# Holding VectorE and ScalarE to program order through the mixer of a hybrid mLSTM and retention block

## The chip, the cores and the metric

The kernel runs on one core of a Trainium2 chip. The time is the device time of one execution in microseconds (us). Of the kernel before there are three runs and one execution taken by the profiler.

The core's engines each work off their own list of instructions, in order: TensorE (PE in the profile; its weight loads are PEld), VectorE (DVE), ScalarE (ACT), GpSimdE (POOL) and SyncE (SP), which here issues the transfers.

## The reference

One layer of a streaming encoder, in fp32, on 1024 tokens of width 1024 with 16 learned meta tokens put in front. Four heads are mLSTM heads (a matrix memory with exponential gates), four are retention heads (rotary q and k, fixed decay). All eight have q and k of 128 columns, v of 256 columns and an output gate of 256 columns.

```
y = rmsnorm(x) @ w_in          # q, k, v, output gates, input and forget gates
mLSTM:     h = (intra-chunk scores * exp gates) @ v + decayed state; then / max(|den|, exp(-m))
retention: h = (q k^T * decay) @ v + q_d @ state; rotary on q and k first
mix = head_norm(h) * sigmoid(gate)   # silu(gate) for retention
x = x + mix @ w_out
out = x + gated MLP(x) with a causal depthwise convolution
```

## The kernel before, in words

Every fp32 product is made of three matmuls on rounded halves: hi times hi, low times hi, hi times low (lines 770 to 772). The halves come from a cast on ScalarE (L363, `hi_..`) and a subtraction on VectorE (L368, `lo_..`). On top of that the big products are done with seven block products in place of eight, so sums of weight blocks are made on VectorE (L441 to L446) and sums of input blocks S1 to S4 are split into halves at L1621 and L1622 (`uS4h`, `uS4l`).

The part between the input norm and the output product is called the mixer here. Head by head, in the order 4, 0, 1, 2, 3, 5, 6, 7, TensorE runs a q/k product (`pq0` and so on), a gate product (`po0`), and for each pair of heads one v product (`pv0`, `pv1`, `pv2`). The first one after the set-up is head 4's gate product `po4`. Each product writes into PSUM banks `x` and `y`, which ScalarE (L838, L840) and VectorE (L842) empty into SBUF several times per product; TensorE's next block needs the bank emptied. Beside the product of one head runs the chunked scan of the head before it: nine chunks of scores `s`, state updates `u`, outputs `n`, then transposes `tr` (L1482) of the normalised outputs, scaled by the gate on VectorE into `mx` (L1490). For the retention heads VectorE and ScalarE also rotate q and k (L1037 to L1042), with tables that are loaded into the buffers A1 and A2 (L964, L965, `A<-rot_d`). Those two buffers held the sum S4's source until the split at L1622 has read it. For the mLSTM heads the gates (L1071 to L1138) are a long chain of small steps on all three engines. In the background, pieces of the output weights are also combined on VectorE (L513 to L517, `raw_w`).

The order of the work is set in two layers. A planner in the Python program (`slot`, `go`, `tick`) emits one piece of TensorE work, then side tasks as long as the estimated load of VectorE and ScalarE is not more than 2.5 us ahead of TensorE's. `watch` (L93) sees each instruction as it is emitted and keeps these estimates in `load`, from a small table of rates. Then a scheduler of the framework reorders each engine's instructions by its own estimate of their timing when the program is built. A manual dependency of the kind NoSync binds two instructions of one engine to the order in which they were emitted, without a semaphore. `watch` makes such a chain where `pinned[0]` is true, and in the kernel before it never is: the lists that the engines get are the scheduler's.

Of the kernel before, what the change touches and what calls it, by code (L numbers as in the profile page):

```python
# [65 lines left out]
def body(ctx, tc, h_in, vecs, cst, mask_in, rot, w_v0, w_vp, w_g, w_out, w_up, w_gate, w_down, out):  # L66
# [18 lines left out]
    G, PE, V, AC = nc.gpsimd, nc.tensor, nc.vector, nc.scalar  # L85
    pinned = [False]
    load = {"PE": 0.0, "DVE": 0.0, "Activation": 0.0, "slot": 0.0}
    RATE = {"PE": (0.004, 0.000445), "DVE": (0.12, 0.00098), "Activation": (0.1, 0.00083)}
    before = {}
# [3 lines left out]
    def watch(ins):  # L93
        nm, kind = ins.engine.name, type(ins).__name__
        if nm not in RATE or not ins.outs or "DMA" in kind or "Tile" in kind:
            return
        if pinned[0] and nm in before:
            tc.add_manual_dep(ins, before[nm], mybir.DependencyInfo(mybir.DependencyClass.NoSync, mybir.DependencyReason.DATA), reason="order")
        before[nm] = ins.name
        b, c = RATE[nm]  # L100
        n = c * math.prod(x[1] for x in ins.outs[0].ap[1:])
        if nm == "Activation":
            f = ins.func.name if hasattr(ins, "func") else "Copy"
            if f in TABLES and f != table[0]:
                table[0] = f
                load[nm] += 1.3
        if nm != "PE":
            load[nm] = max(load[nm], load["slot"]) + b + n
        elif F32 in [x.dtype for x in ins.ins]:
            load[nm] += max(0.11, 2 * n) * (0.5 if ins.outs[0].ap[0][1] == 32 else 2)  # L110
        else:
            load[nm] += max(0.11, b + n)
# [731 lines left out]
    def wino_fm(kind, h, chunks, dst):  # L844
        get = gbanks(f"{kind}{h}")
        steps = []
        for n, (b, xb_) in enumerate(ROWS):
            for ci, (j0, j1) in enumerate(chunks):
                def step(n=n, b=b, xb_=xb_, ci=ci, j0=j0, j1=j1):
                    w = need((kind, h, n))  # L850
                    u = UB[xb_]
                    pt = get(b, ci)[:, :j1 - j0]
                    mm3s(pt, [tuple(x[:, k * P:(k + 1) * P] for x in w) for k in range(4)],
                         [tuple(x[:, k, j0:j1] for x in u) for k in range(4)], n in (0, 1, 3), n in (1, 5, 6))
                    o, d = dst(n, j0, j1)
                    defer(lambda: evac(n, d, pt[:, o:]))
                steps.append(step)
        return steps
# [5 lines left out]
    def fm_dst(tiles, keep=0):  # L864
        def dst(n, j0, j1):
            f, half = QUAD[n]
            o = max(0, 16 - j0) if half else 0
            t0 = half * 512 + j0 + o - keep
            return o, tiles[f][:, t0:half * 512 + j1 - keep]
        return dst  # L870
# [4 lines left out]
    def o_steps(h):  # L875
        return wino_fm("o", h, OC, fm_dst([sigt[:, 0], sigt[:, 1]], KEEP))
# [666 lines left out]
    def slot(m, lim=2.5, most=2, pe=1):  # L1543
        load["slot"] = load["PE"]
        if pend or evacs or front:
            tick()
        m()
        pes = 0
        for _ in range(most):
            if not able() or side[0][1] and pes == pe or max(load["DVE"], load["Activation"]) - load["PE"] > lim:  # L1550
                break
            pes += one()

    def go(steps, pe=1):
        for m in steps:
            slot(m, pe=pe)
# [102 lines left out]
    reset()  # L1659
    load.update({"DVE": 4.0, "Activation": 2.0})  # L1660
    done["tr"] = 0.0
    go(o_steps(4))
    pinned[0] = False
    for p, (a, b) in enumerate(PAIRS):
        side += sig_tasks(prev) if p else sig_tasks(4)
        side += rest[0] + loads_of(a)
# [677 lines left out]
```

## Time and profile before

| | |
|---|---|
| runs | 1553.6, 1558.11, 1556.64 us; median 1556.64 us |
| profiled execution | 1557.89 us, span 1556.1 us |
| TensorE busy | 1503.2 us, 97% of the span |
| VectorE busy | 1076.8 us, 69% |
| ScalarE busy | 772.4 us, 50% |
| mean granted TensorE clock | 0.987 |
| the stretch from the first gate product to the last transposes | about 75 to 746 us from the span's start |

Read it by TensorE's idle time and its clock: an engine at 97% leaves 53 us of idle time in all, and what a change of order can win or lose lies there and in the stretches where the granted clock is below 1.

### The profile page before, as it was taken

Reading aid. Unit: us, or ns where it says so; the run is one execution under the profiler, and the core shown is the slowest. Engines: PE = TensorE matmul, PEld = TensorE weight load, DVE = VectorE, ACT = ScalarE, POOL = GpSimd, SP = SyncE. Lnnn points to the kernel's source line nnn. Section 1 sums busy time; section 2 is a strip of 40 time slices with the busy share of each in tenths; the row PEclk is TensorE's granted clock in tenths of the full one; section 3 lists DMA queues with packets and bytes.
Section 4 is the critical chain, followed back from the end, with each engine's and each line's share of the span. In section 5 each row is a group of like instructions: output and inputs, shape, how many; then the busy total and the mean of one; then the engine's idle time right before and its main releaser. Section 6 shows DMA issues by size and latency. Waiting matters only on the chain.

```text
span 1556.1 us, 25506 instructions
## 1 busy us (share of the span) xinstructions
PE 1503.2 (97%) x9929; PEld 1359.0 (87%) x9929; DVE 1076.8 (69%) x2107; ACT 772.4 (50%) x1467; POOL 73.8 (5%) x133
## 2 busy tenths in 40 slices
PE   7999798999999999999999999999999999999997
PEld 6999698889889999997787988999999999888887
DVE  7785767666677567755767788777666666778657
ACT  5464556664666345635345465444444444444443
POOL 1000000000000000000000001222220000000000
PEclk9999899999999999999999999999999999999999
DMA  6032245323632345489332327888773223933313
GB/s 228 1 109 69 96 114 171 106 86 123 185 115 80 112 154 199 163 304 338 131 109 102 126 71 239 215 204 197 190 190 89 82 82 118 379 119 109 99 43 109
DMA packets 104586, 223.81 MB, mean 144 GB/s; under 512 B 10520, under 2 KB 33760, under 8 KB 104288
## 3 DMA queue, kind: packets, MB, share of 16 engines
q1 hardware_dynamic: 95872, 199.02, 38.7%
q0 software_dynamic: 8448, 23.07, 7.5%
q8 instruction: 78, 1.28, 0.3%
q14 instruction: 44, 0.36, 0.1%
q10 hardware_dynamic: 144, 0.07, 0.0%
HBM read 178.05 MB, written 67.15 MB: 158 GB/s over the span
## 4 chain that ended last, share of the span: by engine, by line
PE 78%; DMA 10%; DVE 8%; ACT 3%; issue 1%; SPq 0%; DVEq 0%; ACTq 0%
PE pdx L772 3%; PE pdx L771 3%; PE pdx L770 3%; PE pup_x L771 2%; PE pup_x L772 2%; PE pup_x L770 2%; PE pga_x L770 2%; PE pga_x L771 2%; PE pga_x L772 2%; DMA raw_w<-w_out_d 2%; PE pdy L772 2%; PE pdy L771 2%; PE pdy L770 2%; PE pwx L772 2%; PE pwx L770 2%; PE pwx L771 2%
## 5 line engine op out<-in xcount | busy, mean ns | idle before, releaser
L654 ACT CAST hi_up<-raw_up 128x512 fp32r<-128x512 f32 (+1 forms) x52 | 36.4, 719 | 107.7 <-PE pga_z L771 61.0
L770 PE MATMUL pup_x<-uh_g,hi_up 128*128 128x256 f32 (+1 forms) x240 | 67.7, 284 | 1.2 <-ACT uh_g L1755 1.2
L771 PE MATMUL pup_x<-ul_g,hi_up 128*128 128x256 f32 (+1 forms) x240 | 67.8, 284 | 0.1
L655 DVE TENSOR_TENSOR lo_up<-raw_up,hi_up 128x512 fp32r<-128x512 f32 (+1 forms) x52 | 41.2, 809 | 37.5 <-ACT hi_up L654 36.8
L655 DVE TENSOR_TENSOR lo_ga<-fraw_ga,hi_ga 128x512 fp32r<-128x512 f32 (+1 forms) x52 | 41.8, 808 | 36.2 <-ACT hi_ga L654 36.1
L772 PE MATMUL pup_x<-uh_g,lo_up 128*128 128x256 f32 (+1 forms) x240 | 66.6, 284 | 0.0
L655 DVE TENSOR_TENSOR lo_d<-rd,hi_d 128x1024 fp32r<-128x1024 f32 (+1 forms) x34 | 37.7, 1112 | 32.8 <-ACT hi_d L654 32.7
L654 ACT CAST hi_ga<-fraw_ga 128x512 fp32r<-128x512 f32 (+1 forms) x52 | 36.5, 719 | 44.1 <-PE pup_z L771 23.1
L772 PE MATMUL pdx<-uh_d,lo_d 128*128 128x512 f32 (+1 forms) x156 | 57.9, 375 | 0.0
L771 PE MATMUL pdx<-ul_d,hi_d 128*128 128x512 f32 (+1 forms) x156 | 57.8, 374 | 0.0
L654 ACT CAST hi_d<-rd 128x1024 fp32r<-128x1024 f32 (+1 forms) x34 | 32.3, 959 | 48.7 <-PE pdy L771 32.5
L772 PE MATMUL pdy<-uh_d,lo_d 128*128 128x512 f32 x132 | 51.9, 393 | 0.0
L771 PE MATMUL pdy<-ul_d,hi_d 128*128 128x512 f32 x132 | 51.8, 392 | 0.0
L770 PE MATMUL pdx<-uh_d,hi_d 128*128 128x512 f32 (+1 forms) x156 | 48.5, 372 | 0.0
L770 PE MATMUL pdy<-uh_d,hi_d 128*128 128x512 f32 x132 | 47.9, 389 | 0.0
L770 PEld LDWEIGHTS pup_x<-uh_g,hi_up 128*128 128x128 f32 x240 | 45.8, 191 | 2.3 <-ACT uh_g L1755 1.4
L770 PE MATMUL pga_x<-uh_g,hi_ga 128*128 128x512 f32 x120 | 47.5, 396 | 0.0
L771 PE MATMUL pga_x<-ul_g,hi_ga 128*128 128x512 f32 x120 | 47.5, 396 | 0.0
L772 PE MATMUL pga_x<-uh_g,lo_ga 128*128 128x512 f32 x120 | 47.2, 393 | 0.0
L771 PEld LDWEIGHTS pup_x<-ul_g,hi_up 128*128 128x128 f32 x240 | 45.8, 191 | 1.0 <-DVE ul_g L1756 0.3
L772 PEld LDWEIGHTS pup_x<-uh_g,lo_up 128*128 128x128 f32 x240 | 45.1, 190 | 0.8
L536 POOL DMA_DIRECT2D wsd<-w_down_d x33 | 18.5, 617 | 483.8 <-DVE s2up L1983 476.9
(1684 smaller groups left out, 5794.2 us busy)
## 6 DMA issues: line engine op xcount, KB each, us to landing
raw_up<-w_up_d SPq DMA_DIRECT2D x22, 512.0 KB, 4.2
fraw_ga<-w_gate_d SPq DMA_DIRECT2D x22, 512.0 KB, 4.1
acts<-cv SPq DMA_DIRECT2D x44, 256.0 KB, 4.3
wsd<-w_down_d POOLq DMA_DIRECT2D x44, 256.0 KB, 6.1
rd<-wsd SPq DMA_DIRECT2D x22, 512.0 KB, 3.5
raw_w<-w_out_d SPq DMA_DIRECT2D x20, 512.0 KB, 4.0
wsw<-raw_w SPq DMA_DIRECT2D x32, 256.0 KB, 2.0
raw_m<-w_out_d SPq DMA_DIRECT2D x14, 512.0 KB, 5.1
```

The source lines that it names most:

```text
L536: dep(G.dma_start(x, y), last["pace"], True)
L654: AC.copy(hi[:, o:o + n], x)
L655: V.tensor_tensor(lo[:, o:o + n], x, hi[:, o:o + n].bitcast(F32), ALU.subtract)
L770: m.append(PE.matmul(pt, ah, xh_, start=first and k == 0, stop=False, skip_group_check=True))
L771: PE.matmul(pt, ah, xl_, start=False, stop=False, skip_group_check=True)
L772: m.append(PE.matmul(pt, al, xh_, start=False, stop=last and k == n - 1, skip_group_check=True))
```

## The change

Three edits in `watch` and around the first gate product. `pinned[0]` becomes true just before head 4's gate product, with the chain started afresh by `before.clear()`, and stays true until the mixer's end, where the line `pinned[0] = dealt[0] = False` stood already. In `watch` the chain leaves TensorE out, so only VectorE and ScalarE (the engines that have a rate there beside PE) are held to the order in which the planner emits; TensorE, and the issue of transfers, stay with the scheduler. And each activation that has more than one input (a bias or scale read from memory) adds 0.15 us to the planner's estimate of ScalarE's load. The instructions are the same but for loads of activation tables, which are placed by the order of ScalarE's functions: 44 in the program before, 31 now. Line numbers of the changed kernel are 2 higher behind `watch`, 3 higher after the call of head 4's gate product.

```diff
--- before.py
+++ after.py
@@ -94,12 +94,14 @@
         nm, kind = ins.engine.name, type(ins).__name__
         if nm not in RATE or not ins.outs or "DMA" in kind or "Tile" in kind:
             return
-        if pinned[0] and nm in before:
+        if pinned[0] and nm in before and nm != "PE":
             tc.add_manual_dep(ins, before[nm], mybir.DependencyInfo(mybir.DependencyClass.NoSync, mybir.DependencyReason.DATA), reason="order")
         before[nm] = ins.name
         b, c = RATE[nm]
         n = c * math.prod(x[1] for x in ins.outs[0].ap[1:])
         if nm == "Activation":
+            if len(ins.ins) > 1:
+                load[nm] += 0.15
             f = ins.func.name if hasattr(ins, "func") else "Copy"
             if f in TABLES and f != table[0]:
                 table[0] = f
@@ -1659,8 +1661,9 @@
     reset()
     load.update({"DVE": 4.0, "Activation": 2.0})
     done["tr"] = 0.0
+    pinned[0] = True
+    before.clear()
     go(o_steps(4))
-    pinned[0] = False
     for p, (a, b) in enumerate(PAIRS):
         side += sig_tasks(prev) if p else sig_tasks(4)
         side += rest[0] + loads_of(a)
```

The first place is VectorE at the start of head 4's gate product. `uS4l` is the low half of S4, whose source lies in the buffers of the rotary tables `A`; `sig<-sig,po4y` empties one of the gate product's banks; `qT`, `kT` and `rawq` with `A` are the rotation of head 4; `pvm` is a small side product. Before:

```order
L1622 TENSOR_TENSOR uS4l<-s_0_849,uS4h 128x1056
L785 TENSOR_TENSOR vz<-pvm_0_1139,vz 16x256
L1075 TENSOR_TENSOR gates<-gates 36x128
L1622 TENSOR_TENSOR uS4l<-s_1_850,uS4h 128x1056
L368 TENSOR_TENSOR lo_o_6_0_977<-raw_o4a,hi_o_6_0_976 128x512
L842 TENSOR_TENSOR sig<-sig,po4y_950 128x256
L785 TENSOR_TENSOR vz<-pvm_0_1139,vz 16x256
L1086 TENSOR_SCALAR gates<-gates 36x128
L368 TENSOR_TENSOR lo_o_6_0_977<-raw_q0a,hi_o_6_0_976 128x512
L1080 TENSOR_SCALAR gates<-gates 36x128
L1040 TENSOR_TENSOR qT_908<-rawq,A_4_877 128x528
L1040 TENSOR_TENSOR qT_908<-rawq,A_4_877 128x512
```

In the changed kernel:

```order
L1624 TENSOR_TENSOR uS4l<-s_0_849,uS4h 128x1056
L1624 TENSOR_TENSOR uS4l<-s_1_850,uS4h 128x1056
L1042 TENSOR_TENSOR qT_908<-rawq,A_4_877 128x528
L1043 TENSOR_TENSOR kT_909<-kT_909,A_4_878 128x528
L1044 TENSOR_TENSOR qT_908<-qT_908,kT_909 128x528
L1073 TENSOR_SCALAR gsm<-vec 36x1
L1075 TENSOR_SCALAR gates<-pg,vec 36x128
L1076 TENSOR_SCALAR gates<-gates 36x128
L1077 TENSOR_TENSOR gates<-gates 36x128
L844 TENSOR_TENSOR sig<-sig,po4y_916 128x258
L1042 TENSOR_TENSOR kT_909<-rawk,A_4_877 128x528
L1043 TENSOR_TENSOR rawq<-rawq,A_4_878 128x528
```

The two splits now stand next to each other with the rotation directly behind them, and the emptying of the bank `po4y_916` stands behind three rows that need the tables and four of the gates. Before, it stood seven rows ahead of the piece shown, and an emptying of the second bank `po4y_950`, weight halves and gate steps stood between the splits and the rotation.

The second place is VectorE in head 1's q/k product. `mx` is the scaled transpose, for which TensorE's next transpose waits; `raw_w` is the combining of output weights. Before:

```order
L842 TENSOR_TENSOR rawq<-rawq,pq1y_2604 128x264
L513 TENSOR_TENSOR raw_w_2676<-raw_w_2676,raw_w_2674 128x512
L1441 BN_STATS bn_8_2551<-v_01_2088 128x6
L514 TENSOR_TENSOR raw_w_2674<-raw_w_2674 128x512
L1456 TENSOR_TENSOR z_2_2571<-den_2006 128x2
L1490 TENSOR_SCALAR mx_0_0_2649<-tr_0_0_2642,vec,sig 128x386
L1442 BN_AGGR mv_2_2509<-bn_8_2551 128x2
L368 TENSOR_TENSOR lo_q_5_0_2602<-raw_q1b,hi_q_5_0_2601 128x512
L368 TENSOR_TENSOR lo_q_5_0_2602<-raw_q1a,hi_q_5_0_2601 128x512
L516 TENSOR_TENSOR raw_w_2674<-raw_w_2674,raw_w_2676 128x512
L1457 TENSOR_TENSOR z_2_2571<-z_2_2571,cols 128x2
```

In the changed kernel:

```order
L370 TENSOR_TENSOR lo_q_5_0_2599<-raw_q1b,hi_q_5_0_2598 128x512
L844 TENSOR_TENSOR rawq<-rawq,pq1y_2621 128x264
L1492 TENSOR_SCALAR mx_0_0_2667<-tr_0_0_2660,vec,sig 128x386
L370 TENSOR_TENSOR lo_q_5_0_2599<-raw_q1a,hi_q_5_0_2598 128x512
L1492 TENSOR_SCALAR mx_0_1_2692<-tr_0_1_2686,vec,sig 128x386
L515 TENSOR_TENSOR raw_w_2646<-raw_w_2646,raw_w_2644 128x512
L516 TENSOR_TENSOR raw_w_2644<-raw_w_2644 128x512
L1492 TENSOR_SCALAR mx_1_0_2717<-tr_1_0_2712,vec,sig 128x384
L518 TENSOR_TENSOR raw_w_2644<-raw_w_2644,raw_w_2646 128x512
L519 TENSOR_TENSOR raw_w_2646<-raw_w_2646,raw_w_2644 128x512
L370 TENSOR_TENSOR lo_o_0_0_2698<-raw_o1a,hi_o_0_0_2697 128x512
```

The first `raw_w` row stood four rows ahead of the first `mx`; now it stands behind the second.

The third place is VectorE at the mixer's end. `wa` and `mm` are the scaled transposes of the last head, `resid` adds output products to the residual. Before:

```order
L1490 TENSOR_SCALAR wa_8267<-tr_1_0_8262,vec,sig 128x258
L1284 TENSOR_TENSOR resid_8121<-resid_8121,pwx_8131 128x512
L1284 TENSOR_TENSOR resid_8121<-resid_8121,pwx_8146 128x512
L1148 TENSOR_TENSOR rr_8351<-wa_8369,rr_8351 128x512
L1284 TENSOR_TENSOR resid_8122<-resid_8122,pwx_8162 128x512
L1284 TENSOR_TENSOR resid_8122<-resid_8122,pwx_8178 128x512
L1490 TENSOR_SCALAR wa_8243<-tr_1_1_8272,vec,sig 128x126
L1490 TENSOR_SCALAR wa_8267<-tr_1_1_8272,vec,sig 128x258
L1247 TENSOR_SCALAR wa_8369<-wa_8369,wa_8389 128x512
L655 TENSOR_TENSOR lo_w_2_8483<-raw_w_2_8280,hi_w_2_8482 128x1024
L1490 TENSOR_SCALAR wa_8267<-tr_2_0_8290,vec,sig 128x254
L1490 TENSOR_SCALAR mm<-tr_2_0_8290,vec,sig 128x2
```

In the changed kernel:

```order
L1492 TENSOR_SCALAR wa_8267<-tr_1_0_8262,vec,sig 128x258
L657 TENSOR_TENSOR lo_w_4_8277<-raw_w_4_8117,hi_w_4_8276 128x1024
L1150 TENSOR_TENSOR rr_8352<-wa_8369,rr_8352 128x512
L1246 TENSOR_SCALAR wa_8369<-wa_8369,wa_8362 128x512
L1492 TENSOR_SCALAR wa_8243<-tr_1_1_8272,vec,sig 128x126
L1492 TENSOR_SCALAR wa_8267<-tr_1_1_8272,vec,sig 128x258
L1150 TENSOR_TENSOR rr_8351<-wa_8369,rr_8351 128x512
L1249 TENSOR_SCALAR wa_8369<-wa_8369,wa_8389 128x512
L1492 TENSOR_SCALAR wa_8267<-tr_2_0_8290,vec,sig 128x254
L1492 TENSOR_SCALAR mm<-tr_2_0_8290,vec,sig 128x2
L1492 TENSOR_SCALAR wa_8267<-tr_2_1_8298,vec,sig 128x254
L1492 TENSOR_SCALAR mm<-tr_2_1_8298,vec,sig 128x2
```

The four `resid` rows between the transposes of the last head are gone from here; they follow behind the last `mm`.

## The prediction

> **What bounds the kernel now.** I read the page first, for the shares of the engines, then the table of TensorE's waits over the stretch that the change touches (75 to 760 us), then the table of stretches for the granted clock, and last the rows in order of time where a wait ends.
>
> ```profile
> span 1556.1 us, 25506 instructions
> PE 1503.2 (97%) x9929; PEld 1359.0 (87%) x9929; DVE 1076.8 (69%) x2107; ACT 772.4 (50%) x1467; POOL 73.8 (5%) x133
> ```
>
> TensorE is the bound: 1556.1 - 1503.2 = 53 us idle in all. VectorE and ScalarE have room on average, so their order matters only where TensorE waits for one of them.
>
> ```profile
> engine line waited for: us in total, times, longest us
> PE tr L1482 <- DVE mx L1490: 8.5, 6, 2.3
> PE tr L1482 <- ACT v4lo L1473: 4.7, 1, 4.7
> PE pq3x L770 <- ACT rawq L838: 2.6, 1, 2.6
> PE pq1x L770 <- ACT rawq L838: 2.2, 1, 2.2
> PE tr L1482 <- DVE mm L1490: 1.8, 1, 1.8
> PE tr L1482 <- DVE wa L1490: 1.8, 1, 1.8
> PE pq2x L770 <- DVE rawk L842: 1.7, 2, 1.3
> PE pq0y L772 <- DVE lo_q L368: 1.6, 1, 1.6
> PE pv0y L770 <- ACT v L840: 0.9, 1, 0.9
> ```
>
> These rows and six smaller ones make 29.6 us of waiting in the mixer: the most that a better order there could win back, apart from the clock.
>
> ```profile
> core 0: us, PE busy (x) PEld busy (x) DVE busy (x) ACT busy (x) POOL busy (x), PEclk, DMA share, GB/s
> 75.00:100.00 25.00, 23.25 (x200) 22.09 (x199) 23.46 (x45) 17.33 (x32) 2.44 (x2) 1.00 0.37 127
> 170.00:180.00 10.00, 3.62 (x12) 2.35 (x13) 9.31 (x21) 7.53 (x12) 0.10 (x1) 0.60 0.13 51
> 180.00:190.00 10.00, 10.00 (x70) 8.94 (x70) 5.50 (x17) 4.21 (x9) 0.32 (x2) 0.89 0.14 47
> 240.00:250.00 10.00, 5.66 (x28) 5.42 (x29) 6.39 (x16) 4.81 (x12) 0.18 (x1) 0.68 0.51 134
> 410.00:420.00 10.00, 6.92 (x47) 6.47 (x46) 5.14 (x16) 6.65 (x19) 0.18 (x1) 0.89 0.64 191
> 420.00:430.00 10.00, 10.00 (x79) 9.86 (x78) 7.31 (x20) 7.14 (x13) 0.00 (x0) 0.94 0.85 286
> 735.00:746.00 11.00, 7.32 (x24) 5.40 (x23) 7.92 (x15) 2.56 (x4) 0.00 (x0) 0.69 0.79 280
> ```
>
> Before PEclk stands the busy time of each engine. The first row matters most: in head 4's gate product VectorE is busy 23.46 of 25 us, so it is nearly the bound there. The others show four places where TensorE's clock falls after a cluster of idle time. With a granted clock of 0.5 in those spells, 0.60 of 10 us means 8 us at half clock, 0.89 means 2.2 us, 0.68 means 6.4, 0.69 of 11 us means 6.8, and 0.89 with 0.94 means 3.4. Half of TensorE's busy time in a spell is lost: by my count of the rows about 2.9 us in head 0's v product, 2.5 in head 1's q/k product (240 to 250), 1.7 in head 3's (410 to 430), 2.8 at the mixer's end.
>
> [...]
>
> **The change part by part.** The instructions stay the same, so each term is a wait that comes or goes. I laid the changed lists of the engines beside each other and put the durations of the rows on them.
>
> *First gate product, a loss.* VectorE now meets the rotation directly behind the split of S4, whose buffers the tables are loaded into.
>
> ```profile
> 81.45 0.41 DVE L842 TENSOR_TENSOR sig<-sig,po4y 128x258 f32<-128x258 f32 x1
> 83.48 1.18 DVE L1622 TENSOR_TENSOR uS4l<-s,uS4h 128x1056 fp32r<-128x1056 f32 x1
> 85.24 1.24 DVE L1622 TENSOR_TENSOR uS4l<-s,uS4h 128x1056 fp32r<-128x1056 f32 x1
> 89.80 1.31 DVE L1040 TENSOR_TENSOR qT<-rawq,A 128x528 f32<-128x528 f32 x2 [0.94 <-DMA A<-rot_d]
> 92.14 0.71 DVE L1041 TENSOR_TENSOR kT<-kT,A 128x528 f32<-128x528 f32 x1 [0.44 <-DMA A<-rot_d]
> 84.74 0.33 SPq L964 DMA_DIRECT2D A<-rot_d  x1
> 86.51 0.33 SPq L965 DMA_DIRECT2D A<-rot_d  x1
> 83.77 0.28 PE L770 MATMUL po4y<-uS1h,hi_o 128*128 128x258 f32 x1
> ```
>
> The tables are issued 0.1 us after each split and land 5.1 and 5.6 us later. Before, VectorE filled that time and waited only 0.94 and 0.44 us; the emptying of `po4y` was done at 81.9, and TensorE used the bank at 83.8. Now nothing stands between: with the splits some 1.7 us earlier (rows moved behind them) the second table lands about 90.4, three steps of 0.7 and four gate steps of about 0.25 follow, and the bank comes free near 92. TensorE has work until about 85.2 (83.8 and one more block of 1.4 us). It waits 6 us. Behind that stand the gate chain between `pe` and `pf` (which has no TensorE work in between now; some ten small steps, which I take as 1.65 us together) and single waits of 1.3, 0.55, 0.45 and 0.7 us: 10.65 us. Then the next weights are late: `raw_q0b` was issued at 87.1 and combined at 95.0, 8 us later with 5.9 us of flight.
>
> ```profile
> 87.11 0.80 SPq L239 DMA_DIRECT2D raw_q0b<-w_g_d  x2
> 95.02 0.68 DVE L441 TENSOR_TENSOR raw_q0b<-raw_q0b 128x512 f32<-128x512 f32 x1
> raw_q0b<-w_g_d SPq DMA_DIRECT2D x2, 256.0 KB, 5.9
> ```
>
> It goes into the slot of `raw_o4a`, and on SyncE it now stands behind the gate tables' transfers as well. By the changed order that slot is read out at about 108, so VectorE waits some 3.7 us for the transfer and TensorE 3 + 1 us. In all 14.65 us idle. For the clock I take 4 us, since a cluster of 8.9 us in head 0's v product cost 2.9. Away go the 1.6 us before `pq0y` and a wait of 0.7. Term: 14.65 + 4.0 - 2.3 = +16.3. Bounds: 0 if the tables land in time, 24 if each wait is half as long again.
>
> *Head 0's v product, a gain.* Before, head 4's scan ends in this product:
>
> ```profile
> 173.15 0.47 PE L1482 MATMUL tr<-cs,v4lo 128*128 128x128 f32 x1 [4.70 <-ACT v4lo L1473]
> 176.90 0.48 PE L1482 MATMUL tr<-cs,v4lo 128*128 128x128 f32 x1 [2.28 <-DVE mx L1490]
> L441 DVE TENSOR_TENSOR raw_vp<-raw_vp,raw_vp 128x1024 f32<-128x1024 f32 x3 | 3.7, 1225 | 6.4 <-DMA raw_vp<-w_vp_d 6.4
> ```
>
> With 1.0 and 0.9 us beside these that is 8.9 us, with the clock 11.8. In the changed order the scan runs beside the q/k product before it, and its transposes are done early in the v product. There the pair L441 and L442 (1.2 us each) stands between two `mx` and ahead of a weight half, which I count as 4.8 us, plus 0.85 for a score that waits for the gate, plus 2.5 of clock: 8.15. Term: -3.7, bounds -11.8 and +4.
>
> *The other two v products, a loss.* Before they idle 3.3 us together with no loss of clock. The same pair of L441 and L442 ahead of an `mx` gives 3.2 us in each now, and 1.7 of clock (one spell of 3.4 us). Term: 9.8 - 3.3 = +6.5, bounds -3.3 and +10.
>
> *Heads 1 and 3, q/k product, a gain.*
>
> ```profile
> L513 DVE TENSOR_TENSOR raw_w<-raw_w,raw_w 128x512 f32<-128x512 f32 x8 | 5.5, 693 | 23.8 <-DMA raw_w<-w_out_d 23.8
> 243.19 0.69 DVE L513 TENSOR_TENSOR raw_w<-raw_w,raw_w 128x512 f32<-128x512 f32 x1 [6.27 <-DMA raw_w<-w_out_d]
> 245.47 0.28 PE L1482 MATMUL tr<-cs,vz 16*128 16x16 f32 x1 [2.25 <-DVE mx L1490]
> ```
>
> VectorE stands 6.27 us before a transfer of output weights with the `mx` of head 1 behind it. The changed order has that `mx` first. ScalarE's `rawq` rows, which TensorE awaited for 2.2 and 2.6 us, now come close together, ahead of the exponentials and their table loads. Before: 2.2 + 2.25 + 2.5 = 7.0 in head 1, and 2.6 + 0.5 + 1.7 = 4.8 in head 3. After, one `mx` row of 0.6 and a little: 0.7 each. Term: -10.4, bounds -11.8 and 0.
>
> *The mixer's end, a gain.* The rows on `wa` and `mm` above, 1.8 us each, are transposes that wait behind residual adds:
>
> ```profile
> 735.46 1.28 DVE L1284 TENSOR_TENSOR resid<-resid,pwx 128x512 f32<-128x512 f32 x2
> ```
>
> With the clock 3.7 + 2.8 = 6.5. The adds now come later, and one wait of about 0.75 stays. Term: -5.7, bounds -6.5 and 0.
>
> *Table loads.* 13 loads of an activation table fall away.
>
> ```profile
> L1461 ACT ACT_TABLE_LOAD x11 | 14.1, 1283 | 0.2
> ```
>
> 13 x 1.283 = 16.7 us of ScalarE, which is idle half of the time: costed at nothing, beyond what the `rawq` rows above hold. The dearer activations only move a few side tasks by one piece of TensorE work: nothing either. TensorE itself is not chained, so its list fits itself to the other two: nothing.
>
> *The other products.* Held to order, VectorE can meet a late transfer with a bank behind it. Bounds: -4 (the small waits of before all go) and +14 (rival two). I take +1, one more wait like the 0.94 us before L1040, which is the same kind of wait.
>
> Sum: 16.3 - 3.7 + 6.5 - 10.4 - 5.7 + 1 = +4.0. The profiled execution took 1557.9 us (span 1556.1 and 1.8 around it), so 1561.9; it stands 1.25 above the median of the three runs, against which the sum gives 1560.6. I forecast 1561. What this kernel's runs can tell from no change is about 0.3%, 4.7 us.
>
> **The rivals.** *One: faster.* The rotary tables land before VectorE needs them, or TensorE gets other work placed there by its free scheduler. The point that decides is whether the second table has landed by about 85, against 92.14 before; for it speaks that 7 us of VectorE's work could still be drawn forward, against it that the split rows themselves set the issue. The gate term then shrinks from 16.3 to about 1, the sum to -11: 1546.
>
> *Two: much slower.* Each of the remaining 11 products gets one in-order wait of about 1.3 us (the banks' emptyings or weight halves behind a transfer; the 23.8 us over eight rows of L513 show how long VectorE can stand there): 14 us in place of 1, so 1574 to 1576. It decides if the planner, which counts the load of engines but sees no transfer's landing, runs ahead of the transfers in the steady heads as well. Against it: `raw_q0b` apart, the weights are issued 8 to 10 us ahead in the changed order, and flights like the 5.9 us above fit in.
>
> *Three: no change.* Terms cancel within 4.7 us, or the scheduler's order was near the planner's anyway: about 1557.
>
> *Four: clock lost only to long gaps.* If idle spells of 1 to 3 us cost no clock, the 2.5, 1.7 and 1.7 us that I count for the changed kernel's three v products fall out of the sum: 1561 - 5.9 = 1555. It decides whether a cluster of short waits is enough; the spell at 240 to 250 us (2.2 and 2.25 us idle, clock 0.68) speaks against it. [...]
>
> **How the numbers follow.** Forecast (1556 to 1567) 0.38, of it 0.24 slower by over 4.7 us and 0.14 within; rival one 0.26, of it 0.25 faster; rival two 0.22, all slower; rivals three and four 0.14, of it 0.09 within and 0.05 faster. Faster 0.30, same 0.24, slower 0.46. The range reaches to both outer rivals, 1546 to 1577; the likeliest case's own range is 1556 to 1567.
>
> **What would show it.** Right: TensorE waits 5 to 7 us on `po4y` near 85 to 92 us with VectorE before it on `A<-rot_d`; a clock below 1 there; `pq0` starting some 10 to 12 us later than the 95.6 us of before's first `pq0y` row; no wait of VectorE on `raw_w` with an `mx` behind it near 240 us; the rows of `tr` on `wa` and `mm` nearly gone. Wrong: no wait on the tables, or waits on `lo_` and bank rows spread through heads 2 to 7.

## The result and the profile after

The changed kernel takes 1625.39 us (median of 4 runs, 1622.98 to 1629.85) against 1556.24 us before (median of 4): a ratio of 1.0449, 95% interval 1.042 to 1.0478. The forecast was 1561, 1546 to 1577. The change is slower by 69 us.

The page of the changed kernel:

```profile
span 1620.8 us, 25436 instructions
PE 1525.0 (94%) x9929; PEld 1373.6 (85%) x9929; DVE 1090.2 (67%) x2107; ACT 751.3 (46%) x1454; POOL 72.0 (4%) x133
```

TensorE's instructions are the same 9929. The span grew by 64.7 us. TensorE's idle time grew from 52.9 to 95.8 us (+42.9), its busy time by 21.8, most of it lost to the clock: the mean granted clock fell from 0.987 to 0.976, about 19 us of work at full clock. ScalarE is 21 us less busy (13 table loads of 1.283 us are 16.7 of it), and the time grew all the same.

TensorE's waits over the mixer (75 to 810 us), the largest:

```profile
engine line waited for: us in total, times, longest us
PE po4y L772 <- DVE sig L844: 10.6, 1, 10.6
PE tr L1484 <- DVE mx L1492: 8.4, 8, 2.3
PE pvm L596 <- DMA raw_vm<-w_vp_d: 8.1, 4, 2.6
PE s L1376 <- DVE pt L1400: 5.5, 4, 4.0
PE pv7y L772 <- ACT v7t L842: 3.6, 1, 3.6
PE pq3y L772 <- ACT rawk L842: 3.1, 1, 3.1
PE pq1y L772 <- ACT rawk L842: 2.9, 1, 2.9
PE pv0x L772 <- ACT hi_vp L365: 2.8, 1, 2.8
PE tr L1484 <- DVE wa L1492: 2.3, 2, 1.5
```

One large wait at the gate product and many small ones spread over all heads. VectorE's three largest waits in the same stretch, and that for `raw_w`:

```profile
engine line waited for: us in total, times, longest us
DVE mx L1492 <- PE tr L1484: 56.1, 27, 3.7
DVE pt L1400 <- ACT kw L1392: 34.1, 22, 4.7
DVE bn L1443 <- ACT v L1439: 33.0, 31, 4.5
DVE raw_w L515 <- DMA raw_w<-w_out_d: 7.9, 4, 3.2
```

The rows on the same things in the kernel before (75 to 800 us):

```profile
DVE raw_w L513 <- DMA raw_w<-w_out_d: 23.8, 8, 6.3
DVE pt L1398 <- ACT kw L1390: 13.6, 14, 2.5
DVE bn L1441 <- ACT v L1437: 8.0, 9, 1.3
DVE wa L1490 <- PE tr L1482: 1.6, 3, 0.8
```

VectorE's row on `tr` before `mx` is new. In the kernel before, VectorE's waits for `tr` come to 1.6 us in all (three rows of `wa` at the end). Now it stands 27 times before an `mx` until TensorE has run the transpose. In these 56.1 us TensorE isn't idle: by the trace it runs matmuls of the products for 47.0 us, and the transposes themselves for most of the rest. The waits for `kw` and `v`, scan results that pass through TensorE and ScalarE, have grown; the wait for the transfers of `raw_w` has shrunk.

By the starts of the products in the two traces, the stages took (us; a stage runs from the first matmul of its product to the first of the next):

| stages | before | after | difference |
|---|---|---|---|
| head 4's gate product, head 0's q/k and v products | 119.3 | 134.4 | +15.1 |
| heads 1 and 3, q/k product | 59.0 | 68.5 | +9.5 |
| the other two v products | 95.9 | 104.5 | +8.6 |
| heads 0 and 2, gate product | 69.8 | 78.5 | +8.7 |
| head 6's and 7's products | 135.2 | 158.8 | +23.6 |
| the others in the mixer | 185.9 | 188.2 | +2.3 |
| all behind the mixer | 816.0 | 813.7 | -2.3 |

How it goes in one place, head 1's q/k product, in order of time on ScalarE, TensorE and VectorE:

```profile
268.67 0.62 ACT L365 CAST hi_o<-raw_o1a 128x512 fp32r<-128x512 f32 x1 [5.03 <-DMA raw_o1a<-w_g_d]
269.20 0.65 ACT L842 ACTIVATE rawk<-pq1y 128x248 f32<-128x248 f32 x2
```

```profile
269.62 0.50 PE L772 MATMUL pq1y<-uS4h,hi_q 128*128 128x264 f32 x1 [2.89 <-ACT rawk L842]
269.92 0.42 PE L773 MATMUL pq1y<-uS4l,hi_q 128*128 128x264 f32 x1
270.14 0.42 PE L774 MATMUL pq1y<-uS4h,lo_q 128*128 128x264 f32 x1
...
273.94 0.28 PE L773 MATMUL pq1y<-uS4l,hi_q 128*128 128x264 f32 x1
274.06 0.28 PE L774 MATMUL pq1y<-uS4h,lo_q 128*128 128x264 f32 x1
274.19 0.49 PE L1484 MATMUL tr<-cs,v 128*128 128x128 f32 x3
```

```profile
274.71 0.62 DVE L1492 SCALAR_TENSOR_TENSOR mx<-tr,vec,sig 128x384 f32<-128x384 f32 x1 [3.71 <-PE tr L1484]
275.25 0.40 DVE L844 TENSOR_TENSOR rawk<-rawk,pq1x 128x248 f32<-128x248 f32 x1
```

ScalarE stands 5.03 us before a cast of weights that are still on their way, with the emptying of `pq1y` behind it. TensorE waits 2.89 us for that bank, then runs the 24 matmuls that its own list has there (the first ones at half clock, 0.22 us from start to start against 0.12 later), and only then the transpose. VectorE, held, waits 3.71 us for this transpose, with the next bank behind it.

Around the single wait of 2.89 us TensorE was busy, and the granted clock was 0.50 from 269.74 to 273.15 us. In the kernel before, with two waits of 2.23 and 2.25 us that ended at 242.09 and 245.47 us, it was 0.50 from 243.62 to 250.45 us.

### The profile page after: what moved, and what is told of

Read it like the earlier page. It is cut to its first block, busy times and chain, and to the rows that moved or that the text cites. A ratio compares the mean times of both kernels' runs of the same rounds, so it can differ in the third digit from the quotient of the medians.

```text
span 1620.8 us, 25436 instructions
## 1 busy us (share of the span) xinstructions
PE 1525.0 (94%) x9929; PEld 1373.6 (85%) x9929; DVE 1090.2 (67%) x2107; ACT 751.3 (46%) x1454; POOL 72.0 (4%) x133
## 4 chain that ended last, share of the span: by engine, by line
PE 82%; DVE 6%; DMA 5%; ACT 4%; issue 1%; SPq 0%; DVEq 0%; ACTq 0%
PE pdx L774 3%; PE pdx L773 3%; PE pdx L772 2%; PE pup_x L773 2%; PE pup_x L774 2%; PE pga_x L772 2%; PE pup_x L772 2%; PE pga_x L773 2%; PE pga_x L774 2%; PE pwx L774 2%; PE pdy L774 2%; PE pdy L773 2%; PE pwx L772 2%; PE pdy L772 2%; PE pwx L773 2%; PE pv L812 2%
## 5 line engine op out<-in xcount | busy, mean ns | idle before, releaser
L1492 DVE SCALAR_TENSOR_TENSOR mx<-tr,vec,sig 128x386 f32<-128x386 f32 (+2 forms) x42 | 24.0, 572 | 60.3 <-PE tr L1484 56.1
```

What stands on the lines that cost most here:

```text
L1492: return V.scalar_tensor_tensor(dst, tr[:, x0 - t0:x1 - t0], vec[:, g:g + 1], sig(b, p)[:, x0 - a0:x1 - a0], ALU.mult, ALU.mult)
```

## The experiments

Theory A: what costs is that the lists of the engines come from two hands, VectorE's and ScalarE's from the planner and TensorE's from the scheduler. Theory B: a held engine stands before whatever lands late, whoever orders TensorE. The diffs are against the changed kernel; where a diff is one line, it stands in place of that line of `watch`. Ratios are to the kernel before, measured beside each, and a loss in us is a median less the median of the kernel before beside it (1553.2 to 1556.2); for the changed kernel it is 69.2 us.

**All three engines held.**

```diff
-        if pinned[0] and nm in before and nm != "PE":
+        if pinned[0] and nm in before:
```

> TensorE is held to the planner's order too, the rest as in the changed kernel (1625.4 us). Theory A, two orders at odds: the changed kernel loses its 69 us mainly because VectorE and ScalarE follow the planner while TensorE follows the scheduler, so VectorE stands before mx for a tr that TensorE runs late (48.4 us of such waits between 200 and 780 us). With one order for all three most of that goes: 1560 to 1585, the 10.6 us wait on po4y at the gate product staying. Theory B, head of line: a held engine stands before whatever lands late, transfers above all, whoever orders TensorE: 1615 to 1640, no better.

Measured 1583.36 us, ratio 1.0195 (1.0173 to 1.0218). The loss is 29.6 us: holding one more engine makes the kernel 40 us faster. VectorE's waits for `tr` (75 to 810 us, as in the view above):

```profile
DVE mx L1492 <- PE tr L1484: 20.8, 17, 2.9
```

56.1 became 20.8. Theory B falls as the main cause; it may stand for part of the 30 us that stay. Against the expectation the wait on `po4y` went too: in its place TensorE waited 14.6 us before `pe`, a step of the gates.

**Only VectorE held.**

```diff
+        if pinned[0] and nm in before and nm == "DVE":
```

> Only VectorE is held, ScalarE and TensorE are free. Theory A: VectorE at tr is the cause, so most of the loss stays: 1600 to 1625. Theory B: the loss splits between the two held engines by their waits on late inputs: about half, 1585 to 1600. Either way the wait on the rotary tables at the gate product stays, about 10 us of TensorE idle near 85 us.

Measured 1613.06 us, ratio 1.0386 (1.0367 to 1.0405): 59 of the 69 us, as theory A said. The wait on `po4y` near 85 us was 5.7 us here and not 10. (In this run the two large weight transfers were issued ahead of both rotary tables; see the last section.)

**Only ScalarE held.**

```diff
+        if pinned[0] and nm in before and nm == "Activation":
```

> Only ScalarE is held. Theory A: little is lost, 1555 to 1570. Theory B: ScalarE stands before casts whose weights land late (5.0 us before hi_o from raw_o1a at 263 us, 5.2 in head 3) with bank rows behind: 1580 to 1600. The two single times of VectorE and ScalarE add up to the 69 us if they act alone, and to much less if they lock each other.

Measured 1554.37 us, ratio 1.0002 (0.9988 to 1.0016): nothing against the kernel before, some 5 us against none held (the next run). The two single losses, 59.3 and 0.6 us, make 60 of the 69. The stages show that this is a sum of a loss and a gain: head 4's gate product and head 0's q/k product 28 us longer, head 0's v product 29 us shorter.

**The dearer activations alone.**

```diff
+        if False:
```

> The dearer activations alone, nothing held to order. Both theories: within 0.3% of the kernel before, 1552 to 1561; the prediction costed this edit at nothing.

Measured 1549.62 us, ratio 0.9977 (0.9966 to 0.9988). The edit by itself is a small gain of about 4 us, and this is the fastest kernel of the study. It leaves 36 table loads of 44, and no single stage gains more than 1.6 us.

**The scaled transposes out of the chain.** Only the rows `mx`, `wa` and `mm` are left to the scheduler.

```diff
-        if pinned[0] and nm in before and nm != "PE":
+        if pinned[0] and nm in before and nm != "PE" and not free[0]:
...
+                free[0] = True
+                r = V.scalar_tensor_tensor(dst, tr[:, x0 - t0:x1 - t0], ...)
+                free[0] = False
```

> As the changed kernel (1625.4 us), but the rows that scale the transposes (mx, wa, mm) are left out of VectorE's chain, so the scheduler places them. Theory A in its narrow form, the mx rows before a late tr are what TensorE pays for: 1580 to 1600. Theory A in its wide form, any row of the held list that reads what TensorE makes late (bank rows, C behind u, pt behind s) does the same: 1605 to 1622, since the other rows stand as before.

Measured 1610.0 us, ratio 1.0361 (1.0326 to 1.0395): a loss of 56.2 us, 13 less. The waits did not go:

```profile
DVE mx L1495 <- PE tr L1486: 51.8, 26, 6.2
```

The narrow form of theory A falls. The place of `mx` in VectorE's list isn't what makes it wait; what makes it wait is how late TensorE runs the transpose: of these 51.8 us TensorE spent 41.9 in matmuls of the products.

**Head 4's rotation held back.**

```diff
         def rotary(i, r):
             a, b = HR[r]
+            while h == 4 and not rush[0] and load["PE"] < 14:
+                yield
```

> As the changed kernel, but the planner holds head 4's rotation back until 14 us of TensorE work of the gate product are planned, so the emptying of the gate product's banks and the next weights stand ahead of the rows that need the tables. The wait of 10.6 us on po4y goes if the tables are its cause. The prediction's gate term says 16 us less: 1606 to 1612. If the gates, which now start as late, only move the wait into head 0's q/k product: 1618 to 1628.

Measured 1617.43 us, ratio 1.0411 (1.0382 to 1.044): a loss of 63.7 us, 5.5 less than the changed kernel (8 by the bare medians): between the two expectations and nearer the second. The wait on `po4y` is gone and head 4's gate product takes 22.4 us in place of 38.8, so the tables were its cause. But head 0's v product then takes 5.9 us more and its gate product 7.4 us more: of the 16.4 us most came back in later stages.

**The chain only into head 0's v product.** The line stands behind the first 13 of that product's 28 steps, so the chain ends in the middle of it, not at its end, where the expectation below puts it.

```diff
         drain(f"V{p}")
+        pinned[0] = False
```

> The chain ends at the end of head 0's v product, the rest of the mixer is left to the scheduler. This measures what the part up to head 0's second gate product costs by itself: by the stages of the two traces 15 us (134.4 against 119.3 us), so 1565 to 1573, and 50 to 55 us of the loss lie in the heads after it. If the late heads only suffer from the late start: 1595 or more.

Measured 1566.29 us, ratio 1.0087 (1.0053 to 1.012): a loss of 12.5 us, in the lower part of what was expected. Some 57 us lie behind.

**The chain only from behind head 4's gate product.**

```diff
-    pinned[0] = True
-    before.clear()
     go(o_steps(4))
+    pinned[0] = True
+    before.clear()
```

> The chain starts only after head 4's gate product. With 12.5 us measured for the chain up to head 0's v product alone, the rest of the 69 us stays if the parts add: 1605 to 1615, a little less if head 0's gains in the v product were part of the 12.5. If the start sets the heads off their pace for good: under 1590.

Measured 1611.68 us, ratio 1.0375 (1.0338 to 1.0413): the loss stays without the start, 58.5 us. With the 12.5 of the run above that is 71, against 69: the two parts add. Both hold head 0's q/k product and the first part of its v product, so this is a rough sum.

**TensorE and VectorE held, ScalarE free.**

```diff
+        if pinned[0] and nm in before and nm != "Activation":
```

> TensorE and VectorE are held, ScalarE is free. Theory A, the pair of TensorE and VectorE must have one order and ScalarE's matters little: 1575 to 1592, as with all three held (1583.4 us). If the three orders must all be one, so that a free ScalarE does to the pair what a free TensorE did: 1600 or more.

Measured 1587.1 us, ratio 1.022 (1.0188 to 1.0252): as with all three. ScalarE's order matters little.

**Only TensorE held.**

```diff
+        if pinned[0] and nm in before and nm == "PE":
```

> Only TensorE is held to the planner's order, VectorE and ScalarE are free. If any two orders at odds cost as much as the changed kernel's: 1590 or more. If it is a held VectorE that costs, since TensorE is the bound and the scheduler can fit the others to it: 1545 to 1565, near the kernel with the dearer activations alone (1549.6).

Measured 1585.42 us, ratio 1.0206 (1.0175 to 1.0237). Neither expectation holds. The planner's order of TensorE alone costs 32 us, and holding the other two as well adds nothing (29.6). Its waits are of another kind: TensorE waits for `mx`, hardly VectorE for `tr` (75 to 810 us; TensorE's view first, then VectorE's).

```profile
PE tr L1484 <- DVE mx L1492: 26.3, 13, 6.8
PE pe L1101 <- DVE gates L1094: 14.0, 1, 14.0
```

```profile
DVE mx L1492 <- PE tr L1484: 5.1, 7, 1.1
```

Theory A as first put falls with this run: here too the lists come from two hands, and it costs no more than one. What costs 40 us more is a held VectorE beside a free TensorE.

**All held but the product matmuls.**

```diff
-        if pinned[0] and nm in before and nm != "PE":
+        if pinned[0] and nm in before and not free[0]:
...
     def mm3s(pt, a, x, first, last):
+        free[0] = True
...
+        free[0] = False
         return m[0], m[-1]
```

> VectorE and ScalarE are held as in the changed kernel, and of TensorE the small rows (scores, states, outputs, transposes, gate sums) are in one chain with them; the matmuls of the products stay free to overtake. If product matmuls that overtake a transpose are what VectorE pays for: 1600 to 1625, no better than the changed kernel. If the order among the small rows is what matters: 1580 to 1592, as with all of TensorE held (1583.4).

Measured 1608.0 us, ratio 1.0352 (1.0326 to 1.0378). Holding the scan's rows and transposes of TensorE among themselves brings back 14 of the 40 us that holding all of TensorE does (losses of 54.8, 69.2 and 29.6), and VectorE's wait for the transposes stays whole:

```profile
DVE mx L1496 <- PE tr L1488: 57.1, 25, 5.9
```

In these 57.1 us TensorE ran matmuls of the products for 48.4. The other 25 of the 40 us come when the products' matmuls are held too. So VectorE waits for the product matmuls that stand ahead of a transpose in TensorE's own list. This form of theory A is the one that the runs leave standing. How such a wait comes back as idle time of TensorE is seen in single places (head 1's above, the second v product's below) and not added up over the mixer.

**All held, rotation held back.** The edits of the first and of the sixth run together.

> All three engines held, and head 4's rotation held back as in the run before with two engines (there it gave 8 us). The wait of 14.6 us before pe goes; by the stages, all held loses 10 us up to head 0's second gate product, so 1573 to 1580; if it only moves into the next stages: 1580 to 1585.

Measured 1584.93 us, ratio 1.0204 (1.0174 to 1.0234), no gain over all held. The wait before `pe` fell from 14.6 to 7.5 us, head 0's v product took 19 us more: it only moved, as the second expectation had it.

The runs that hold one engine or several stand together as follows (ratio to before, all with the dearer activations):

| held | ratio |
|---|---|
| none | 0.9977 |
| ScalarE | 1.0002 |
| TensorE | 1.0206 |
| VectorE | 1.0386 |
| VectorE, ScalarE (the change) | 1.0449 |
| TensorE, VectorE | 1.0220 |
| all three | 1.0195 |

Against none held, the planner's order costs 2.2 to 2.4% when TensorE takes part in it, with or without the others. With VectorE held and TensorE left out it costs 4.1 to 4.7%. A free TensorE is no help to a held VectorE; it costs 1.7 to 2.5 points more.

## Why the prediction was wrong

**The step that failed** is the sentence "TensorE itself is not chained, so its list fits itself to the other two: nothing". The scheduler's list for TensorE does not fit the held VectorE on the chip: VectorE waits 56.1 us for transposes, 47.0 of them while TensorE runs matmuls of the products, and holding TensorE to the same order takes 40 us off. I had laid the changed lists beside each other and put durations on them stage by stage, but started each stage with TensorE on its time. Small delays carry: late weights, an emptying behind the cast, half clock, a late transpose, the next emptying behind that.

**Other products**, taken as +1 with +14 as the far end, were about 34 us in the trace (the rows of the stage table that no other term names). This term took the direction of rival two, in-order waits through the heads, but at more than twice its price. The sign of being wrong that the prediction names came with it: TensorE waited 2.1 to 3.6 us each on bank and `lo_` rows of heads 2, 3 and 7 (`po2y`, `po3x`, `pq3y`, `pv7y`). My bound rested on one mechanism, VectorE before a late transfer; its wait for `raw_w`, from which I priced that, fell from 23.8 to 7.9 us.

**First gate product and head 0's v product**, +16.3 - 3.7 = +12.6: by the stages +15.1, by the run that ends the chain inside that v product 12.5 us. Right in kind, and near in sum in part by luck, since two misses run against each other: TensorE's idle time grew by 15.7 us in the gate and q/k products (12.4 forecast) and fell by 4.8 in the v product (3.3 forecast). The wait on `po4y` was 10.6 us and not 6. Of the 4.6 us between them 2.3 lie in my own sum: from a table at 90.4, three steps of 0.7 and four of 0.25 end at 93.5 and not near 92, 8.3 us after 85.2. The other 2.3 are the second table, there at 92.65 and not at 90.4. It took 8.5 us to land (issued 84.14), with two weight transfers issued between the tables on SyncE.

```profile
85.66 0.71 DVE L1042 TENSOR_TENSOR qT<-rawq,A 128x528 f32<-128x528 f32 x1 [3.36 <-DMA A<-rot_d]
92.65 0.71 DVE L1043 TENSOR_TENSOR kT<-kT,A 128x528 f32<-128x528 f32 x1 [6.29 <-DMA A<-rot_d]
121.94 0.69 DVE L443 TENSOR_TENSOR raw_q0b<-raw_q0b 128x512 f32<-128x512 f32 x1 [5.70 <-DMA raw_q0b<-w_g_d]
```

The wait for `raw_q0b` came, 5.7 us on VectorE (some 3.7 forecast) and 4.0 on TensorE as forecast (the row on `pt` above). Head 0's q/k product began 17.6 us later than before by the two traces, against 10 to 12 forecast.

**Heads 1 and 3, q/k product**, forecast -10.4: +9.5. The first `raw_w` rows did go behind the first two `mx`, but in head 1 VectorE still waited 2.92 us for one of them ahead of the third `mx`. The transposes there wait little for `mx`. A new wait came, that on `rawk` (2.9 and 3.1 us), behind ScalarE's cast before late weights. I had named the emptyings and the exponentials on ScalarE's list, and not looked at which transfer the cast ahead of them needs.

**The other two v products**, forecast +6.5: +8.6, right in kind too. In each, the pair of sums on `raw_vp` stands between two `mx`, and TensorE waits 2.3 us behind it, with half clock after that (granted 0.50 from 361.90 to 365.31 and from 546.22 to 549.63 us). In the second v product, VectorE's rows first, then TensorE's:

```profile
356.35 0.62 DVE L1492 SCALAR_TENSOR_TENSOR mx<-tr,vec,sig 128x384 f32<-128x384 f32 x1 [2.79 <-PE tr L1484]
356.89 1.22 DVE L443 TENSOR_TENSOR raw_vp<-raw_vp,raw_vp 128x1024 f32<-128x1024 f32 x1
358.14 1.23 DVE L444 TENSOR_TENSOR raw_vp<-raw_vp,raw_vp 128x1024 f32<-128x1024 f32 x1
359.28 0.48 DVE L1492 SCALAR_TENSOR_TENSOR mx<-tr,vec,sig 128x256 f32<-128x256 f32 x1
```

```profile
359.81 0.44 PE L1484 MATMUL tr<-cs,v 128*128 128x128 f32 x2 [2.29 <-DVE mx L1492]
```

VectorE stands 2.79 us until TensorE has run a transpose, runs the pair late for it, and TensorE then stands 2.29 us before the next `mx`.

**The mixer's end**, forecast -5.7: the last stage took 35.8 us against 34.8, so no gain. The residual adds are out of the way, but transposes still waited 2.3 us for `wa`, and other waits came in their place.

**Table loads**: 13 fewer, nothing gained that shows, as forecast; the run with ScalarE alone held has the same 31 and takes the time of the kernel before. The **dearer activations** were costed at nothing and gave about -4 us, inside the 0.3% bound.

**Rival four**, clock lost only to long gaps, is contradicted by the 2.89 us wait shown above, behind which the matmuls ran at half clock (granted 0.50 for 3.41 us). **Rival one** needed the second table by about 85 us; it was there at 92.65.

What stays open: why the planner's order costs 2.2% by itself even with all engines in it. Head 6's gate product (34.7 us against 25.6 before) and head 7's (36.9 against 31.3) hold half of it by the trace with all three held, and the stages up to head 0's v product another 10.4 us. The late heads were not tried by themselves. In head 6's gate product TensorE idles 4.4 us there (0 before), longest 1.9 us for a weight half `lo_o`, and the mean granted clock is 0.90 over 34.7 us, 3.4 us of work at full clock. That makes 7.8 of the 9.1 us. Why that half is late, and where head 7's 5.6 us come from, is open. A part of theory B may live there.

## What to carry to other kernels

Where a scheduler writes the lists of several engines together, fixing the list of one engine and leaving free the one whose results it waits for is not a milder form of fixing all: here VectorE and ScalarE held beside a free TensorE cost 40 us more than all three held, and leaving all free was best. When lists are compared by hand, carry each delay into the next stage, and look for what every row at the head of a held engine waits for, a transfer, a bank or a transpose, before counting on what stands behind it.

## What the runs showed of the hardware that was not expected

The time that the rotary tables took to land differed between the runs, and so did what was issued just ahead of them on SyncE. In the three runs with two transfers of 512 KB issued between the two rotary tables of 520 KB (the changed kernel, the scaled transposes left free, the chain only into head 0's v product), the second table took 8.5, 9.0 and 8.3 us. Where those two were issued 1.3 us ahead of the first table (only VectorE held), both tables took 6.9 to 7.0 us. In the kernel before, where they were issued 2.8 us ahead of the first, the tables took 5.0 and 5.6, and in the nine other runs, with nothing or 256 KB transfers between the tables, 4.4 to 5.8. No run changes this order alone, so the cause is not separated.

And in the changed kernel half clock came behind single waits of TensorE between busy work: behind the one of 2.89 us, 3.41 us at a granted clock of 0.50 (269.74 to 273.15 us), and behind one of 1.69 us that ended at 971.88 us, after the mixer, 3.41 us as well (972.89 to 976.30 us).
